# A hybrid encoder block on one core: which projection units are computed as seven half-size products, and what runs beside them

## The chip, the cores and the metric

The kernel runs on one core of a Trainium2 chip. The metric is the device time of one execution in microseconds (us), as the median of several runs. The engines are TensorE (PE, matmuls), VectorE (DVE), ScalarE (ACT), GpSimd (POOL) and SyncE (SP, here the queue that issues all DMAs). Each works through its own list of instructions in order and waits on semaphores for the others.

## The reference, cut to what matters

```python
h = rmsnorm(x, norm_w)                                   # 1024 tokens x 2048
q_a, k_a, v_a, g_a, q_r, k_r, v_r, g_r = split(h @ w_in) # 1024, 256, 256, 1024, 512, 512, 1024, 1024 columns
attn = windowed_attention(q_a, k_a, v_a, sink, rel_bias) # 16 heads of 64, window of 128
attn = rmsnorm(attn, attn_out_norm_w) * silu(g_a)
ret  = bidirectional_retention(rotary(q_r), rotary(k_r) / 8, v_r, decays)  # 8 heads, chunks of 128
ret  = head_groupnorm(ret, ret_gn_w) * silu(g_r)
x    = rmsnorm(x + concat(attn, ret) @ w_out, final_norm_w)
```

All is float32. The kernel splits each operand of the two large products into a high and a low part (float32r) and adds three matmuls, high x high, high x low and low x high.

## The kernel before, in words

The input projection is cut into units of 256 output columns for all 1024 tokens. There are 22: one of attention's keys (`ka`), one of its values (`va`), four of its queries (`qa`), four of retention's queries and keys (`qk`, 128 columns of each), four of retention's values (`vr`), four of attention's gates (`ga`) and four of retention's gates (`gr`).

The six units in `STD` (L26) are computed plainly (loop at L922): 16 steps over the inner dimension, at each four PSUM banks with three matmuls of 512 columns each (L973 to L975), 192 in all. The value unit has the tokens as the stationary operand and 256 columns as the moving one, so 384 matmuls (L966 to L968), and its result stands with tokens in the partitions. Units use the banks Ma and Mb, except the third and fifth, which use ST and O. `evac` (L852) takes a bank out of PSUM.

The 16 units in `FAST` (L27) are computed as seven half-size products in the manner of Strassen and Winograd: a half of the inner dimension is treated as a 2 x 2 block product, with combined tokens in `hT` and combined weights made on the fly. One pass over all 16 units takes the first half of the inner dimension, a second pass the second half (the loop at L1153, 32 half-units, each of seven slots p = 0 to 6 with 12 matmuls, L1035 to L1037, so 84). Slots of neighbouring units interleave: (q,0), (q-1,4), (q,1), (q-1,6), (q,2), (q-1,5), (q,3). For a slot `prep` splits weights (ACT the high part at L159, POOL the low part at L153), `prep_sums` combines them (on POOL in the first pass, on DVE in the second), and `collect` (L1050) takes the banks: bank a after products 0, 2, 4 and 5, b after 1, c after 4 and again after 6. In the first pass the first use of a bank is an ACT copy, in the second a DVE add to the partial sum, which the first pass stored to DRAM (`yd`) and which is loaded again. Between the passes `hT` is reloaded row by row (`c_load`, `c_split`).

A finished half-unit of the second pass goes through `deliver` (L1082). Gates get SiLU. Queries and keys are rotated (`rope`, L1105: a DVE shuffle, a POOL product, a DVE product, a DVE add), with two loads of cosine and sine. Values of retention are turned by four PE transposes into token order (`to_tokens`, L1123) and copied by ACT. Both are put off by a slot through the list `later`.

Everything else is done in pieces beside these matmuls. After every 3 matmuls of a product or bank (6 in a value unit), `point()` (L235) counts on; each `pace` points it runs one step of the queue `jobs` (attention's four groups, L494, then retention's four jobs, L648), each `apace` points one step of `aux` (bias copies, attn_sum, premix), and each point one step of `post`. Attention begins beside the last plain unit (L938) and goes on beside the first pass. Retention begins in the second pass, at slot 2 of its third unit (L1178). Its state chain is `kv` (L694, `scalar_tensor_tensor` at L156 into the tile ST). `premix` (L817) multiplies attention's gates with the norm's factors (POOL, L827) and its outputs (DVE, L830). The output projection follows in eight units (L1220), the first of them still beside retention's end.

A store is put off by seven points (`store`, L99) so that the SP queue does not wait for its data. Small tiles come from a ring of six (`t2`).

Of the kernel before, what the change touches and what calls it, by code (L numbers as in the profile page):

```python
# [21 lines left out]
NT2 = 6  # L22
# [14 lines left out]
def hybrid_block(ctx: ExitStack, tc: tile.TileContext, a: dict, out: bass.AP):  # L37
# [61 lines left out]
    def store(dst, src, t, then=None, delay=7):  # L99
# [5 lines left out]
        pend.append((pt[0] + delay, go, serial[t.name]))  # L105

    def held(t, bufs):
        tag, n = serial[t.name]

        return t  # L110

# [120 lines left out]

    pt, due, pace, adue, apace = [0], [0], [2.9], [0], [2.0]

# [242 lines left out]
    def q_post(i, tiles):  # L477
        for b, t in enumerate(tiles):
            et, hf = b // 2, b % 2
            for part in range(2):  # L480
                x = t2(F32R)
                if part == 0:
                    A.copy(x, t)
                    hi = x
                else:
                    tt(V, x, t, hi.bitcast(F32), ALU.subtract)
                last = (lambda: done.add(("qa", i))) if b == 3 and part else None
                store(qsd[2 * i + et, part, :, 512 * hf : 512 * hf + 512], x.bitcast(F32), x, last)
            yield

# [351 lines left out]
    def mixed_row():  # L842
# [6 lines left out]
        split(orow(row, 0), orow(row, 1), r)  # L849


    def evac(u, b, p, st):  # L852
        kind, i = STD[u]
        hf = b % 2
        d = t2()
        if kind == "va":
            for z in range(2):
# [4 lines left out]
                else:  # L862
                    A.activation(dz, pz, AF.Copy, scale=c)
            for z in range(2):
# [17 lines left out]
    def c_split(r):  # L882
        split(hT[:, r, 0:512], hT[:, r, 512:1024], held(staged.pop(r), NT2))

# [37 lines left out]
    for u, (kind, i) in enumerate(STD):  # L922
# [5 lines left out]
        for pos in range(NK):  # L928
# [29 lines left out]
            for b in range(4):  # L958
                p = banks[b]
                if kind == "va":  # L960
                    for z in range(2):
# [23 lines left out]
        elif kind == "qa":  # L985
            post.append((q_post(i, st), None))


# [50 lines left out]

    later = deque()  # L1040

    def partial(q, b):
# [36 lines left out]

    count = {}  # L1080

    def deliver(q, b):  # L1082
# [8 lines left out]
        def finished():  # L1091
            count[kind, i] = count.get((kind, i), 0) + 1
            if count[kind, i] == 4:
                done.add((kind, i))

        if kind in ("ga", "gr"):
            A.activation(t, t, AF.Silu)
            c = (0 if kind == "ga" else 8) + 2 * i + et
            store(gd[128 * c : 128 * c + 128, sl], t, t, finished)
        elif kind == "qk":  # L1100
            cs, sn = t2(), t2()
            SP.dma_start(cs, a["cos"][:, sl])
            SP.dma_start(sn, a["sin"][:, sl])

            def rope():  # L1105
                sh = t2()
                V.stream_shuffle(sh, t, [z ^ 1 for z in range(32)])
                tt(G, t, t, cs, ALU.mult)
                tt(V, sh, sh, sn, ALU.mult)

                def add():
                    tt(V, t, t, held(sh, NT2), ALU.add)
                    store(rqk[i, et, :, sl], t, t, finished)

                if q == NF:
                    add()
                else:
                    later.append(add)

            later.append(rope)  # L1120
        else:

            def to_tokens():  # L1123
                p = pT()
                for c in range(4):
                    T.transpose(p[:, 128 * c : 128 * c + 128], t[:, 128 * c : 128 * c + 128], ident)
                o = t2()
                A.copy(o, p)
                dst = vrd[i, :, 4 * hf : 4 * hf + 4, 128 * et : 128 * et + 128]
                store(dst, o.rearrange("p (c e) -> p c e", c=4), o, finished)  # L1130

            later.append(to_tokens)

# [19 lines left out]
    for n, (q, p) in enumerate(slots):  # L1153
# [8 lines left out]
        multiply(q, p)  # L1162
        now, ready_fns = later, list(later)
        later.clear()
        collect(q, p)
        for f in ready_fns:
            f()

# [7 lines left out]
        if q == NF - 1:  # L1176
            coming.extend(4 * p + j for j in range(4))
        if (q, p) == (NF + 2, 2):  # L1178
            drain(jobs, ("attn", 3))
# [5 lines left out]
            done.add("ret")  # L1185
            pace[0], apace[0] = 3.5, 3.0
            for g in range(4):
# [22 lines left out]
    assert mix_next[0] == 14, mix_next  # L1210
    while later:
        later.popleft()()
    while mixing:
# [235 lines left out]
```

## Time and profile before

| | |
|---|---|
| median of 3 runs | 1595.64 us (1592.18 to 1596.6) |
| profiled execution | 1595.88 us, its span 1594.1 us |
| mean granted clock of TensorE | 0.975 |
| DMA | 311.73 MB, mean 196 GB/s |

The span runs from the first to the last instruction; what lies around it is 1.8 us. A group's row gives line, engine, operation and tile, then busy time and the mean of one, then the idle time before it and what ended it. A row of the timeline begins with its start in us and its length; in brackets stands the idle time of the engine ahead of it and the releaser. PE's matmuls are pipelined: the length of one is longer than the distance of two starts.

### The profile page before, as it was taken

The page shows a single profiled execution, that of the slowest core. Times are in us where ns is not written, and L with a number is a line of the kernel's source. Part 1 is how long each engine was busy: PE and PEld are TensorE (multiplying, and loading weights), DVE is VectorE, ACT ScalarE, POOL GpSimd, SP SyncE. Part 2 cuts the span into 40 slices and gives each one's busy share as a digit, 9 for nine tenths or more (in the row PEclk, how much of TensorE's full clock was granted, in tenths as well). Part 3 has the DMA queues.
Part 4 walks back from the last instruction along what each step waited for, and adds up shares of the span by engine and source line. Part 5 has one row for each costly group of instructions (what it writes and reads, how often), then busy time and mean ns, then how long its engine had stood idle before and what let it go on. Part 6 is the DMA issues. An engine that isn't in the chain of part 4 may idle for free. (4 is left out here: it accounts for less than half of the span.)

```text
span 1594.1 us, 21805 instructions
## 1 busy us (share of the span) xinstructions
PE 1484.5 (93%) x7250; PEld 1237.2 (78%) x7250; DVE 923.5 (58%) x1880; ACT 668.1 (42%) x1417; POOL 591.0 (37%) x457
## 2 busy tenths in 40 slices
PE   8999998999999999998888698879998999999997
PEld 6998877887888888887777577657777787887886
DVE  6655446854564664577747856867667444364323
ACT  5311136764675675774332232222353343333210
POOL 3232221446556556445645545554442000113000
PEclk9999999999999999999999899989999999999999
DMA  8888668775455556357774675675464565566413
GB/s 302 300 268 296 243 187 276 244 235 161 139 160 154 159 162 189 115 160 247 242 232 142 201 242 175 219 252 163 155 230 150 173 224 185 159 206 199 135 35 106
DMA packets 195405, 311.73 MB, mean 196 GB/s; under 512 B 29355, under 2 KB 67243, under 8 KB 194652
## 3 DMA queue, kind: packets, MB, share of 16 engines
q1 hardware_dynamic: 195292, 310.33, 60.0%
q8 instruction: 57, 0.93, 0.3%
q14 instruction: 56, 0.46, 0.1%
HBM read 216.38 MB, written 93.88 MB: 195 GB/s over the span
## 5 line engine op out<-in xcount | busy, mean ns | idle before, releaser
L153 POOL TENSOR_TENSOR wl<-r,wh 128x512 fp32r<-128x512 f32 x224 | 298.7, 1337 | 318.9 <-ACT wh L159 308.3
L159 ACT CAST wh<-r 128x512 fp32r<-128x512 f32 x224 | 138.3, 619 | 194.4 <-PE psMa L1036 82.7
L1035 PE MATMUL psMa<-hT,wh 128*128 128x512 f32 x512 | 213.1, 416 | 5.8 <-DVE e L153 4.0
L1037 PE MATMUL psMa<-hT,wl 128*128 128x512 f32 x512 | 201.7, 394 | 2.3 <-POOL wl L153 2.3
L1035 PE MATMUL psMb<-hT,wh 128*128 128x512 f32 x384 | 166.0, 432 | 38.8 <-DVE e L153 38.7
L1036 PE MATMUL psMa<-hT,wh 128*128 128x512 f32 x512 | 201.0, 393 | 0.0
L159 ACT CAST wh<-e 128x512 fp32r<-128x512 f32 x160 | 97.9, 618 | 216.7 <-PE psMb L1254 78.7
L153 DVE TENSOR_TENSOR wl<-e,wh 128x512 fp32r<-128x512 f32 x112 | 84.6, 761 | 132.4 <-ACT wh L159 127.9
L1036 PE MATMUL psMb<-hT,wh 128*128 128x512 f32 x384 | 157.6, 410 | 0.0
L1037 PE MATMUL psMb<-hT,wl 128*128 128x512 f32 x384 | 157.2, 409 | 0.0
L153 POOL TENSOR_TENSOR wl<-e,wh 128x512 fp32r<-128x512 f32 x48 | 71.9, 1501 | 203.8 <-ACT wh L159 203.8
L1035 PEld LDWEIGHTS psMb<-hT,wh 128*128 128x128 f32 x384 | 77.4, 202 | 56.0 <-issue 32.2
L1035 PEld LDWEIGHTS psMa<-hT,wh 128*128 128x128 f32 x512 | 96.9, 189 | 24.6 <-issue 3.4
L1037 PEld LDWEIGHTS psMa<-hT,wl 128*128 128x128 f32 x512 | 96.7, 189 | 24.4 <-POOL wl L153 2.7
L560 DVE CUSTOM_DVE_ANT_0 P<-psST,bias,nsink 128x384 f32<-128x384 f32 (+1 forms) x128 | 74.1, 580 | 62.7 <-PE psST L552 62.4
L1036 PEld LDWEIGHTS psMa<-hT,wh 128*128 128x128 f32 x512 | 97.3, 190 | 16.0
L153 DVE TENSOR_TENSOR PTl<-psST,PTh 128x384 fp32r<-128x384 f32 (+1 forms) x128 | 66.7, 521 | 45.5 <-ACT PTh L604 42.4
L153 POOL TENSOR_TENSOR r<-r,r 128x512 f32<-128x512 f32 x64 | 85.0, 1329 | 20.8 <-DMA yd<-e 6.7
L159 ACT CAST hT<-t 128x512 fp32r<-128x512 f32 x100 | 60.6, 620 | 72.0 <-DMA t<-in_w_out 25.5
L1037 PEld LDWEIGHTS psMb<-hT,wl 128*128 128x128 f32 x384 | 76.8, 200 | 17.7
L564 ACT ACTIVATE P<-P,nmx 128x385 f32<-128x385 f32 (+1 forms) x128 | 76.1, 594 | 30.5 <-DVE nmx L560 28.9
L153 DVE TENSOR_TENSOR e<-psMb,e 128x512 f32<-128x512 f32 x96 | 65.6, 686 | 38.9 <-PE psMb L1037 32.4
(335 smaller groups left out, 3530.3 us busy)
## 6 DMA issues: line engine op xcount, KB each, us to landing
r<-in_w_fast SPq DMA_DIRECT2D x128, 256.0 KB, 2.8
e<-in_w_out SPq DMA_DIRECT2D x112, 256.0 KB, 2.9
yd<-e SPq DMA_DIRECT2D x64, 256.0 KB, 2.9
e<-yd SPq DMA_DIRECT2D x64, 256.0 KB, 3.5
t<-in_xT SPq DMA_DIRECT2D x31, 512.0 KB, 6.1
t<-cd SPq DMA_DIRECT2D x56, 256.0 KB, 4.3
e<-in_w_in SPq DMA_DIRECT2D x48, 256.0 KB, 4.7
md<-t SPq DMA_DIRECT2D x48, 256.0 KB, 2.8
```

What stands on the lines that cost most here:

```text
L153: eng.tensor_tensor(o, x, y, op)
L159: A.copy(o_hi, x)
L560: V.tensor_tensor_reduce(x[:, :W], p[:, :W], bias[2 * pr + c][:, k0 : k0 + W], -1.0, nsink[:, head : head + 1], ALU.add, ALU.min, nmx[:, c ...
L564: A.activation(x[:, : W + 1], x[:, : W + 1], AF.Exp, bias=nmx[:, c : c + 1], scale=-1.0, accum_out=sums[:, c : c + 1])
L1035: T.matmul(bank, wh[:, ws], hh, start=(j == 0 and p in (0, 1, 3)), stop=False, skip_group_check=True)
L1036: T.matmul(bank, wh[:, ws], hl, start=False, stop=False, skip_group_check=True)
L1037: T.matmul(bank, wl[:, ws], hh, start=False, stop=(j == 3), skip_group_check=True)
```

## The change

`qk` and `vr` move from `FAST` to `STD`. There are now 14 plain units and eight units of seven products, the gates alone, so 16 half-units instead of 32. The four `qk` units are plain with 192 matmuls, the four `vr` units like the value unit with 384 matmuls of 256 columns, in token order from the start, so that the transposes go. The rotation is a generator in the queue `post` (`rope_post`), with one load at a time through the single buffer e22; the store of retention's values stands in `evac`. Attention begins beside the same unit as before (`U_ATT`), now followed by eight more plain units, one step each 3.1 points instead of 2.9. Retention begins at slot 2 of the second half-unit of the first pass, one step each 3.3 points instead of 3.5, and premix takes a step each 2.0 points instead of 3.0. The parts of the diff:

```diff
 STD = [("ka", 0), ("va", 0), ("qa", 0), ("qa", 1), ("qa", 2), ("qa", 3)]
-FAST = []
 for _p in range(4):
-    FAST += [("qk", _p), ("vr", _p)]
-    FAST += [("ga", 2 * _p), ("ga", 2 * _p + 1)] if _p < 2 else []
-FAST += [("gr", _p) for _p in range(4)]
+    STD += [("qk", _p), ("vr", _p)]
+FAST = [("ga", _p) for _p in range(4)] + [("gr", _p) for _p in range(4)]
+U_ATT = 5
...
-    pt, due, pace, adue, apace = [0], [0], [2.9], [0], [2.0]
+    pt, due, pace, adue, apace = [0], [0], [3.1], [0], [2.0]
...
+    def rope_post(i, tiles):
+        for b, t in enumerate(tiles):
+            et, hf = b // 2, b % 2
+            sl = slice(512 * hf, 512 * hf + 512)
+            cs = et_("e22")
+            SP.dma_start(cs, a["cos"][:, sl])
+            for _ in range(4):
+                yield
+            sh = t2()
+            V.stream_shuffle(sh, t, [z ^ 1 for z in range(32)])
+            tt(G, t, t, cs, ALU.mult)
+            sn = et_("e22")
+            SP.dma_start(sn, a["sin"][:, sl])
+            for _ in range(5):
+                yield
+            tt(V, sh, sh, sn, ALU.mult)
+            tt(V, t, t, sh, ALU.add)
+            store(rqk[i, et, :, sl], t, t, lambda: one_more("qk", i))
+            yield
...
-        if kind == "va":
+        if kind in ("va", "vr"):
...
+            if kind == "vr":
+                dst = vrd[i, :, 2 * b : 2 * b + 2, :]
+                store(dst, d.rearrange("p (c e) -> p c e", c=2), d, lambda: one_more("vr", i))
...
-            if last_u and pos == 0:
+            if u == U_ATT and pos == 0:
...
-        if kind in ("ga", "gr"):
-            A.activation(t, t, AF.Silu)
-            c = (0 if kind == "ga" else 8) + 2 * i + et
-            store(gd[128 * c : 128 * c + 128, sl], t, t, finished)
-        elif kind == "qk":
...
-        else:
-
-            def to_tokens():
-                p = pT()
-                for c in range(4):
-                    T.transpose(p[:, 128 * c : 128 * c + 128], t[:, 128 * c : 128 * c + 128], ident)
...
+        A.activation(t, t, AF.Silu)
+        c = (0 if kind == "ga" else 8) + 2 * i + et
+        store(gd[128 * c : 128 * c + 128, sl], t, t, finished)
...
-        if (q, p) == (NF + 2, 2):
+        if (q, p) == (1, 2):
...
-            pace[0], apace[0] = 3.5, 3.0
+            pace[0], apace[0] = 3.3, 2.0
```

Two places in the order of the instructions. The first is PE beside attention. Before, in the first pass, attention's scores (L551, L552 into psST) and values (L582, L583 into psO) stand between two groups of three matmuls of a half-size product (L1035 to L1037):

```order
L1035 MATMUL psMb_2980<-hT,wh_2917 128x512
L1036 MATMUL psMb_2980<-hT,wh_2917 128x512
L1037 MATMUL psMb_2980<-hT,wl_2918 128x512
L551 MATMUL psST_2984<-k_314_2133,qj_2794 128x384
L552 MATMUL psST_2984<-k_315_2134,qj_2794 128x384
L582 MATMUL psO_2999<-PTh_2886,k_316_2135 128x256
L583 MATMUL psO_2999<-PTl_2887,k_316_2135 128x256
```

In the changed kernel the same (now L565, L566, and the transposes of the weights P, L611) stand between groups of a unit of retention's values (L991 to L993):

```order
L993 MATMUL psMb_3418<-wh_3879,hT 128x256
L565 MATMUL psST_4072<-k_619_3514,qj_3778 128x384
L566 MATMUL psST_4072<-k_620_3515,qj_3778 128x384
L611 MATMUL psST_4079<-ident,P_3900 128x128 x3
L991 MATMUL psMb_3419<-wh_3879,hT 128x256
L992 MATMUL psMb_3419<-wl_3880,hT 128x256
L993 MATMUL psMb_3419<-wh_3879,hT 128x256
```

Attention has moved from beside half-size products to beside plain units, whose matmuls here have 256 columns.

The second is DVE at retention's state chain (ST). Before, in the second pass, sums of weights (r) and adds of both banks (from psMa and psMb) stand among its steps:

```order
L156 SCALAR_TENSOR_TENSOR ST_8969<-ST_8969,cdec 64x128
L153 TENSOR_TENSOR e_1914_8937<-psMa_8680,e_1914_8937 128x512
L156 SCALAR_TENSOR_TENSOR ST_8969<-ST_8969,cdec 64x128
L153 TENSOR_TENSOR e_1914_8937<-psMb_8899,e_1914_8937 128x512
L156 SCALAR_TENSOR_TENSOR ST_8969<-ST_8969,cdec 64x128
L153 TENSOR_TENSOR r_8989<-r_8746,r_8989 128x512
L156 SCALAR_TENSOR_TENSOR ST_8969<-ST_8969,cdec 64x128
L153 TENSOR_TENSOR e_1905_8897<-psMb_9035,e_1905_8897 128x512
```

In the changed kernel the first chain stands in the first pass (L150 is the state step, L724 its copy, L147 the two-operand operations, sd retention's weighted scores):

```order
L150 SCALAR_TENSOR_TENSOR ST_8919<-ST_8919,cdec,psST_8914 64x128 x4
L147 TENSOR_TENSOR e_1604_8754<-psMb_8788,e_1604_8754 128x512
L147 TENSOR_TENSOR sd_8950<-psST_8945,dt_8798 128x512
L724 COPY ST_8919<-psST_8962 64x512
L150 SCALAR_TENSOR_TENSOR ST_8919<-ST_8919,cdec,psST_8962 64x128
L150 SCALAR_TENSOR_TENSOR ST_8919<-ST_8919,cdec 64x128
L150 SCALAR_TENSOR_TENSOR ST_8919<-ST_8919,cdec,psST_8962 64x128
L150 SCALAR_TENSOR_TENSOR ST_8919<-ST_8919,cdec 64x128
```

The adds from psMa and the sums of r are not on DVE there; the add from psMb is.

More of the change, by code (lines that the diff above doesn't have):

```diff
@@ L849, in mixed_row, with one_more @@
         split(orow(row, 0), orow(row, 1), r)
+    count = {}
+    def one_more(kind, i):
+        count[kind, i] = count.get((kind, i), 0) + 1
+        if count[kind, i] == 4:
+            done.add((kind, i))
     def evac(u, b, p, st):
@@ L863, in evac @@
                     A.activation(dz, pz, AF.Copy, scale=c)
-            for z in range(2):
+            for z in range(2) if kind == "va" else ():
                 store(
@@ L959, in hybrid_block @@
                 p = banks[b]
-                if kind == "va":
+                if kind in ("va", "vr"):
                     for z in range(2):
@@ L986, in hybrid_block @@
             post.append((q_post(i, st), None))
+        elif kind == "qk":
+            post.append((rope_post(i, st), None))
     raws, sums, ready_w, banks, outs = {}, {}, {}, {}, {}
```

38 lines of the change are left out of this document (2 added, 36 removed).

## The prediction

> **What bounds the kernel now.** I read the page's head first, then the table of stages, then the waits of the worst stage, then the timeline at its longest waits. The head gives span and busy time:
>
> ```profile
> span 1594.1 us, 21805 instructions
> PE 1484.5 (93%) x7250; PEld 1237.2 (78%) x7250; DVE 923.5 (58%) x1880; ACT 668.1 (42%) x1417; POOL 591.0 (37%) x457
> ```
>
> TensorE (PE) sets the time. Its busy time counts each matmul to its modelled end, so I take its pace from starts. The rows are the last matmul of the value unit and the first of the next plain unit, and that unit's last and its successor's first; then the first two of the value unit (256 columns each), and a run of four 128-column transposes with the matmul behind it:
>
> ```profile
> 101.82 0.28 PE L968 MATMUL psMb<-wh,r 128*128 128x256 f32 x1
> 101.94 0.40 PE L973 MATMUL psST<-hT,wh 128*128 128x512 f32 x1
> ...
> 145.26 0.39 PE L975 MATMUL psO<-r,wl 128*128 128x512 f32 x1
> 145.49 0.39 PE L973 MATMUL psMa<-hT,wh 128*128 128x512 f32 x1
> ...
> 52.56 0.28 PE L966 MATMUL psMa<-wh,hT 128*128 128x256 f32 x1
> 52.68 0.28 PE L967 MATMUL psMa<-wl,hT 128*128 128x256 f32 x1
> ...
> 1056.65 0.66 PE L1126 MATMUL psST<-ident,e 128*128 128x128 f32 x4 [1.22 <-DVE e L153]
> 1057.06 0.48 PE L1035 MATMUL psMa<-hT,wh 128*128 128x512 f32 x1
> ```
>
> A plain unit of 192 matmuls of 512 columns takes 145.49 - 101.94 = 43.55 us, 0.2268 us a matmul. A matmul of 256 columns takes 0.12 us, a transpose 0.41 / 4 = 0.10 us. Half a gate unit, one pass of seven products with 84 matmuls, needs 84 x 0.2268 = 19.05 us if nothing stands in the way.
>
> The table of stages has, in order: the value unit, a plain unit, the plain unit beside which attention begins, the first pass (16 half-units, beside attention), the first half-unit of the second pass, the whole second pass (beside retention), its last four half-units (gates only), the first output unit, and the rest. Columns are length, busy time of each engine, granted clock, DMA share and GB/s.
>
> ```profile
> 52.56:101.94 49.38, 49.25 (x403) 48.06 (x402) 33.07 (x44) 11.84 (x22) 18.32 (x10) 1.00 0.75 251
> 101.94:145.49 43.55, 43.55 (x194) 36.06 (x193) 17.92 (x25) 5.70 (x10) 10.75 (x8) 1.00 0.93 310
> 235.90:301.73 65.83, 60.96 (x313) 50.89 (x312) 45.16 (x116) 45.20 (x106) 11.72 (x9) 1.00 0.84 268
> 301.73:740.36 438.63, 423.50 (x2186) 360.08 (x2184) 252.73 (x655) 280.94 (x667) 244.42 (x187) 0.99 0.54 169
> 740.36:762.09 21.73, 19.37 (x84) 15.71 (x85) 19.29 (x24) 11.33 (x21) 13.66 (x10) 1.00 0.85 279
> 740.36:1213.60 473.24, 408.55 (x1961) 334.58 (x1962) 332.57 (x599) 155.90 (x296) 234.86 (x180) 0.94 0.63 206
> 1101.40:1213.60 112.20, 102.83 (x523) 85.28 (x522) 77.27 (x169) 48.59 (x93) 44.56 (x36) 0.97 0.55 183
> 1213.60:1274.10 60.50, 57.08 (x282) 46.80 (x281) 30.43 (x84) 21.82 (x43) 6.74 (x6) 0.97 0.50 158
> 1274.10:1594.10 320.00, 307.06 (x1345) 251.39 (x1343) 136.58 (x234) 96.61 (x194) 26.66 (x24) 0.99 0.48 156
> ```
>
> The second pass is the bad stage: PE stands idle for 473.24 - 408.55 = 64.7 us of it and is granted 0.94 of its clock, against 15.1 us and 0.99 in the first pass. DVE, not POOL, is the busiest helper there (70%). PE's waits in the second pass, by what it waited for (total, times, longest):
>
> ```profile
> PE psMb L1035 <- DVE e L153: 35.7, 9, 5.7
> PE psST L1126 <- DVE e L153: 22.5, 7, 7.7
> PE psMa L1035 <- DVE e L153: 4.0, 3, 2.8
> ```
>
> The first row is one place. Bank c is read by DVE after product 4 and written again by product 6, with only product 1 of the next half-unit between. When DVE has other work, PE stands. That work is retention's state chain, here ahead of a 5.70 us wait:
>
> ```profile
> 878.21 0.87 DVE L156 SCALAR_TENSOR_TENSOR ST<-ST,cdec 64x128 f32<-64x128 f32 x1
> 879.11 0.34 DVE L156 SCALAR_TENSOR_TENSOR ST<-ST,cdec,psST 64x128 f32<-64x128 f32 x1
> 879.48 0.35 DVE L156 SCALAR_TENSOR_TENSOR ST<-ST,cdec 64x128 f32<-64x128 f32 x1
> 879.87 0.69 DVE L153 TENSOR_TENSOR e<-psMa,e 128x512 f32<-128x512 f32 x1
> ...
> 880.97 0.69 DVE L153 TENSOR_TENSOR e<-psMb,e 128x512 f32<-128x512 f32 x1
> ...
> 881.81 0.77 PE L1035 MATMUL psMb<-hT,wh 128*128 128x512 f32 x1 [5.70 <-DVE e L153]
> ```
>
> **More matmuls.** Eight units become plain. Each saved 2 x 19.05 = 38.1 us as half-size products. Four query-key units now cost 43.55: 4 x 5.45 = 21.8 us more. Four value units cost 384 matmuls of 256 columns; 384 x 0.12 = 46.1 us by the starts, and the value unit's whole row, 49.38, is the upper end (19 other matmuls stand in it). I take 46.1: 4 x 8.0 = 32.0 us more. Their 64 transposes go: 64 x 0.10 = 6.6 us less. The sum is 47.2 us more work for PE, which nothing hides. The Trainium skill (TensorE: Matmul & The Clock Gate, Back-to-back issue gap) gives N / 2.4 ns plus about 2.5 ns from one warm matmul to the next: 215.8 ns for 512 columns, 109.2 for 256, so an estimate of 4 x 5.2 + 4 x 5.7 - 6.6 = 37 us. The rows' 226.8 and 120 ns are longer, and this chip's rows stand.
>
> **Attention beside plain units.** The stage ran from 235.90 to 740.36, 504.5 us: a plain unit, 16 x 19.05 = 304.8, and 156.1 left for attention's own matmuls with all delays. Attention's matmuls stay. What the half-size products added to the delays goes. Its prices are a bank wait, and the first matmul of each group of three, whose mean is 416 and 432 ns against 393 and 410 for the second:
>
> ```profile
> PE psMb L1035 <- DVE e L153: 6.2, 2, 3.2
> ...
> L1035 PE MATMUL psMa<-hT,wh 128*128 128x512 f32 x512 | 213.1, 416 | 5.8 <-DVE e L153 4.0 <-ACT e L1059 1.3 <-DVE bmv L748 0.5
> L1036 PE MATMUL psMa<-hT,wh 128*128 128x512 f32 x512 | 201.0, 393 | 0.0
> ```
>
> 448 groups in the first pass x 22 ns is 9.9, with 6.2 makes 16: 140 us stay. At best 25 go (131). At worst nothing goes and something comes: units follow one another on the same four banks, and the rotation (rope_post) puts 16 tiles of shuffle, product and add on DVE, with a POOL product and two loads through a single buffer between. A wait of that kind, in the second pass: a DVE operation 3.87 us late behind POOL, which was 5.50 us late behind a load:
>
> ```profile
> 961.17 1.29 POOL L153 TENSOR_TENSOR t<-t,t 128x512 f32<-128x512 f32 x1 [5.50 <-DMA t<-rbd]
> ...
> 962.49 1.77 DVE L156 SCALAR_TENSOR_TENSOR t<-t,ew,t 128x512 f32<-128x512 f32 x1 [3.87 <-POOL t L153]
> ```
>
> DVE is idle 42% of the first pass, so PE should see little of it; 1 us a tile as the upper end gives 156 + 16 = 172. As the order of PE in the section on the change shows, attention's pieces are the same; only what lies between them changes.
>
> Stage: 5 x 43.55 + 4 x 46.1 + 140 = 542.2 us, to 778.1.
>
> **Retention beside both passes.** Rotation, transposes and their stores leave these passes, and with them a wait on SP, whose queue holds the loads of weights and partial sums behind a store that waits for its data (SP's waits in the second pass); the rewritten store of retention's values now waits for its eviction beside attention, where weights are loaded 16 matmul groups ahead:
>
> ```profile
> SPq L101 <- ACT t L1128: 14.4, 7, 7.4
> ...
> r<-in_w_fast SPq DMA_DIRECT2D x128, 256.0 KB, 2.8
> ...
> yd<-e SPq DMA_DIRECT2D x64, 256.0 KB, 2.9
> e<-yd SPq DMA_DIRECT2D x64, 256.0 KB, 3.5
> ```
>
> Of the three kinds of transfers half go (64, 32 and 32 of 256 KB), and 64 loads of plain weights come, for a DMA share of 0.63: I cost that at nothing. The nearest row is the last four half-units before, gates with retention: 112.20 / 4 = 28.05 us each. About 13.5 half-units have retention beside them (four jobs of 29 steps, 3.3 points apart, 28 points to a half-unit). In the first pass DVE loses four sums and four adds a half-unit, as POOL makes the sums and ACT copies: in the order of DVE shown with the change, the adds from psMa and the sums of r are gone from between the state steps, the adds from psMb stay. Eight operations of 0.69 us are 5.5 us off DVE; I take 2 us of it for PE, 26.0 a half-unit, bounds 24.5 (midway between the 21.73 of the half-unit without retention and the first pass's mean, 438.63 / 16 = 27.4) and 29.6 (473.24 / 16). The pass: 6.7 x 26.0 + 6.8 x 28.05 + 2.5 without retention x 21.73 = 419.3. To this come 4 for reloading hT beside retention, 3 for the change from attention (the 2.8 us wait above), and 8 for premix, whose 16 pieces now stand two points a step instead of three, so that loads have less time (bounds 0 and 16). 434.3 us, to 1212. The bounds are 398 (24.5 and 26.0 a half-unit, and of the extras only the 3) and 481 (16 x 29.6, and 8). Retention then ends inside the pass, and the first output unit is plain: 43.55 + 1.5 = 45 instead of 60.50.
>
> **Sum.** 235.9 + 542.2 + 434.3 + 45 + 320.0 = 1577.4 us span. The profiled execution took 1595.88 us with a span of 1594.1, and the median of the runs is 1595.64, so the span lacks 1.8: 1579 us, 1.1% faster. A measurement of this kernel tells about 0.3% from nothing.
>
> **Rivals.** *Retention costs the same wherever it lies* (ends slower). The first pass gives POOL four sums more a half-unit. In the rows above a state step of 0.35 us took 0.87, and a three-operand product 1.77; undisturbed it takes 0.74:
>
> ```profile
> 861.73 0.74 DVE L156 SCALAR_TENSOR_TENSOR t<-t,ew,t 128x512 f32<-128x512 f32 x1
> L153 POOL TENSOR_TENSOR r<-r,r 128x512 f32<-128x512 f32 x64 | 85.0, 1329 | 20.8 <-DMA yd<-e 6.7 <-DMA r<-in_w_fast 6.4 <-issue 3.0
> ```
>
> If a POOL operation of 1.33 us holds DVE, the chain before bank c grows again by what the adds gave back: 16 x 29.6 + 8 = 481, 1626 us. It decides from about 28.3 us a half-unit with retention. The Trainium skill (SBUF — State Buffer, Who interferes with whom) says that a VectorE operation with two SBUF inputs and a GpSimd one that reads SBUF exclude each other for the whole instruction; the 0.74 and 1.77 us agree. 25%. *The plain units give it back*: attention keeps all its delays (156 us), 1595 us: 13%. For it speaks the rotation's single buffer, against it DVE's idle 42%. *Both stages run near their floor*: 131 and 398, 1534 us: 15%; for it speaks the 21.73 us of a half-unit without retention, against it the chain that stays. That the change does not do what it says is excluded by the order.
>
> **Numbers.** The forecast has 47%; of it 2 lie within 0.3%. Faster 0.45 + 0.15 = 0.60; within 0.3% 0.12 + 0.02 = 0.14; slower 0.25 + 0.01 = 0.26. The range, 1550 to 1618, leaves out the outer half of the floor rival and of the slower one.
>
> **What would show it.** Right: the stage from 235.9 ends near 778, half-units with retention last 26 to 28 us, the L1126 waits are gone, the psMb waits on DVE fall from 35.7 to some 20 us, the first output unit takes 45. Wrong: half-units over 28.3 in the first pass, or the attention stage past 795.

## The result and the profile after

The changed kernel takes 1647.4 us (median of 1642.42, 1647.4 and 1651.24; with one further, slow execution of 5238.3 us the median would be 1649.3), the kernel before 1593.9 us beside it. The ratio is 1.0334, with a 95% interval of 1.029 to 1.0379: slower by 53 us, where 1579 us was forecast, with a range of 1550 to 1618. The profiled execution took 1651.24 us, its span 1649.5.

```profile
span 1649.5 us, 23105 instructions
PE 1533.6 (93%) x8146; PEld 1310.8 (79%) x8146; DVE 840.6 (51%) x1800; ACT 625.6 (38%) x1337; POOL 480.7 (29%) x377
```

DVE lost 83 us of work (923.5 before), POOL 110, ACT 43. PE's 49 us more of busy time came through in full, and 6 more (by the spans). The table of stages of the changed kernel, with the columns of before: attention beside nine plain units, the last of these units, the first pass, in it half-units 2 to 7 (counted from 0; retention beside them), the second pass, in it half-units 8 to 14, and the first output unit.

```profile
237.40:807.60 570.20, 539.87 (x3474) 493.49 (x3472) 289.69 (x794) 269.95 (x660) 140.40 (x107) 0.97 0.50 154
736.80:807.60 70.80, 55.43 (x444) 54.52 (x442) 40.51 (x68) 30.62 (x61) 29.03 (x21) 0.90 0.76 242
807.60:1028.30 220.70, 199.36 (x989) 165.13 (x989) 102.90 (x237) 82.64 (x164) 133.86 (x107) 0.96 0.43 142
851.40:1028.30 176.90, 155.56 (x789) 128.87 (x787) 94.74 (x220) 66.01 (x132) 101.39 (x83) 0.96 0.42 138
1028.30:1277.70 249.40, 211.78 (x981) 169.43 (x982) 169.00 (x319) 96.23 (x185) 112.36 (x87) 0.92 0.67 222
1028.30:1249.60 221.30, 189.67 (x897) 151.91 (x897) 148.83 (x292) 81.88 (x161) 104.98 (x82) 0.93 0.64 211
1277.70:1327.50 49.80, 46.65 (x194) 37.82 (x193) 20.54 (x32) 16.65 (x30) 0.00 (x0) 0.93 0.60 192
```

| term | forecast | measured | surplus |
|---|---|---|---|
| to the start of attention | 235.9 | 237.4 | 1.5 |
| attention stage | 542.2 | 570.2 | 28.0 |
| both passes | 434.3 | 220.7 + 249.4 = 470.1 | 35.8 |
| first output unit | 45 | 49.8 | 4.8 |
| the rest | 320.0 | 322.0 | 2.0 |
| span | 1577.4 | 1649.5 | 72.1 |

Half-units 2 to 7 last 176.9 / 6 = 29.5 us (26.0 forecast), 8 to 14 last 221.3 / 7 = 31.6 (28.05, with 12 us of extras besides). All that is not plain, half-size or output matmuls at their own pace took, between the start of attention and the end of the first output unit, 504.5 + 533.74 - 696.7 = 341.5 us before, and takes 1090.1 - 750.5 = 339.6 now (the matmuls: 2 x 43.55 + 32 x 19.05 = 696.7, and 6 x 43.55 + 4 x 46.1 + 16 x 19.05 = 750.5). The forecast had it fall to 271. It did not fall: that is the whole error but 3.5 us. (6.6 us of the 341.5 were the transposes that went.)

What waited in both passes (engine, tile and line, what for; total, times, longest):

```profile
PE psMb L1062 <- DVE e L147: 27.9, 7, 7.4
DVE bnt L147 <- POOL bny L147: 24.5, 15, 6.5
DVE t L150 <- POOL t L147: 23.1, 8, 5.5
POOL t L147 <- DMA t<-rbd: 20.3, 7, 5.1
PE psMa L1062 <- ACT e L1084: 8.4, 2, 6.1
PE psMa L1062 <- DVE e L147: 8.2, 2, 6.4
```

The waits of L1126 are gone and psMb's fell from 35.7, both as forecast; others stand in their place. In the first pass, the timeline of POOL, DVE, ACT and PE about one of them:

```profile
915.53 1.29 POOL L147 TENSOR_TENSOR r<-r,r 128x512 f32<-128x512 f32 x1
916.89 2.39 POOL L147 TENSOR_TENSOR qs<-rq,qd 64x1024 f32<-64x1024 f32 x1
919.36 1.28 POOL L147 TENSOR_TENSOR r<-r,r 128x512 f32<-128x512 f32 x1
...
921.11 1.26 POOL L147 TENSOR_TENSOR wl<-r,wh 128x512 fp32r<-128x512 f32 x1
922.33 1.02 POOL L147 TENSOR_TENSOR bny<-bnv,mhalf 128x4 f32<-128x4 f32 x1
...
915.80 1.04 DVE L765 TENSOR_SCALAR bnv<-bmv 128x4 f32<-128x4 f32 x1
923.38 0.16 DVE L147 TENSOR_TENSOR bnt<-bnv,bny 128x4 f32<-128x4 f32 x1 [6.54 <-POOL bny L147]
...
924.43 0.88 ACT L777 ACTIVATE on<-on,bnt,bny 128x128 f32<-128x128 f32 x2 [8.38 <-DVE bnt L150]
...
926.46 0.57 ACT L1084 COPY e<-psMa 128x512 f32<-128x512 f32 x1
...
920.64 0.39 PE L1064 MATMUL psMb<-hT,wl 128*128 128x512 f32 x1
927.08 0.79 PE L1062 MATMUL psMa<-hT,wh 128*128 128x512 f32 x1 [6.05 <-ACT e L1084]
```

Four queues in a row: POOL's power for the group norm (bny, four columns) has its operand at 916.8 and stands behind a product (qs), a sum (r) and a split (wl) until 922.3; DVE waits for it 6.54 us with nothing else, ACT 8.38 us for DVE, ACT's copy of the bank stands behind, and PE waits 6.05 us for the bank. In the second pass premix does the like: POOL's product waits for a load, DVE for POOL, PE for the DVE add behind:

```profile
1146.44 1.26 POOL L147 TENSOR_TENSOR t<-t,t 128x512 f32<-128x512 f32 x1 [5.07 <-DMA t<-rbd]
...
1147.73 1.73 DVE L150 SCALAR_TENSOR_TENSOR t<-t,ew,t 128x512 f32<-128x512 f32 x1 [5.50 <-POOL t L147]
...
1150.21 0.77 PE L1062 MATMUL psMb<-hT,wh 128*128 128x512 f32 x1 [5.52 <-DVE e L147]
```

### The profile page after: what moved, and what is told of

Its sections match the earlier page's. It is cut to its first block, busy times and chain, and to the rows that moved or that the text cites. A ratio compares the mean times of both kernels' runs of the same rounds, so it can differ in the third digit from the quotient of the medians.

```text
span 1649.5 us, 23105 instructions
## 1 busy us (share of the span) xinstructions
PE 1533.6 (93%) x8146; PEld 1310.8 (79%) x8146; DVE 840.6 (51%) x1800; ACT 625.6 (38%) x1337; POOL 480.7 (29%) x377
## 4 chain that ended last, share of the span: by engine, by line
PE 52%; DMA 15%; DVE 12%; issue 10%; POOL 6%; ACT 3%; SPq 1%; POOLq 0%; ACTq 0%; DVEq 0%
DMA t<-gd 3%; POOL wl L147 2%; PE psMa L998 2%; PE psMa L999 2%; PE psMa L1000 2%; PE psMb L998 2%; PE psMb L999 2%; PE psMb L1000 2%; DMA e<-in_sin 2%; PE psMa L1062 2%; DVE ST L150 2%; DMA t<-cd 2%; PE psMa L1063 2%; PE psMa L1064 2%; PE psST L611 2%
## 5 line engine op out<-in xcount | busy, mean ns | idle before, releaser
L147 POOL TENSOR_TENSOR wl<-e,wh 128x512 fp32r<-128x512 f32 x112 | 155.7, 1392 | 519.5 <-ACT wh L153 509.6
L147 POOL TENSOR_TENSOR wl<-r,wh 128x512 fp32r<-128x512 f32 x112 | 149.8, 1341 | 171.2 <-ACT wh L153 164.3
L147 DVE TENSOR_TENSOR wl<-e,wh 128x512 fp32r<-128x512 f32 x112 | 84.2, 757 | 138.6 <-ACT wh L153 134.5
L1062 PE MATMUL psMa<-hT,wh 128*128 128x512 f32 x256 | 107.7, 421 | 22.6 <-ACT e L1084 8.4
L1062 PE MATMUL psMb<-hT,wh 128*128 128x512 f32 x192 | 83.7, 436 | 28.4 <-DVE e L147 27.9
L153 ACT CAST wh<-r 128x512 fp32r<-128x512 f32 x112 | 68.8, 618 | 104.6 <-PE psMa L1063 61.9
L1064 PE MATMUL psMa<-hT,wl 128*128 128x512 f32 x256 | 102.6, 401 | 0.0
L1063 PE MATMUL psMa<-hT,wh 128*128 128x512 f32 x256 | 102.6, 401 | 0.0
L147 DVE TENSOR_TENSOR PTl<-psST,PTh 128x384 fp32r<-128x384 f32 (+1 forms) x128 | 66.9, 523 | 51.5 <-ACT PTh L618 47.3
L147 DVE TENSOR_TENSOR hT<-t,hT 128x512 fp32r<-128x512 f32 x84 | 68.5, 832 | 40.7 <-ACT hT L153 39.0
L998 PE MATMUL psMa<-hT,wh 128*128 128x512 f32 x196 | 81.2, 414 | 6.2 <-DVE hT L287 6.2
L991 PE MATMUL psMa<-wh,hT 128*128 128x256 f32 x280 | 81.6, 291 | 0.0
L991 PE MATMUL psMb<-wh,hT 128*128 128x256 f32 x280 | 81.3, 290 | 0.0
L998 PE MATMUL psMb<-hT,wh 128*128 128x512 f32 x196 | 80.6, 411 | 0.0
L992 PE MATMUL psMb<-wl,hT 128*128 128x256 f32 x280 | 80.4, 287 | 0.0
L993 PE MATMUL psMb<-wh,hT 128*128 128x256 f32 x280 | 80.3, 287 | 0.0
L992 PE MATMUL psMa<-wl,hT 128*128 128x256 f32 x280 | 80.2, 287 | 0.0
```

The costliest lines, as they stand in the source:

```text
L147: eng.tensor_tensor(o, x, y, op)
L153: A.copy(o_hi, x)
L991: T.matmul(po, hh, wh[:, ws], start=first and z == 0, stop=False, skip_group_check=True)
L992: T.matmul(po, hh, wl[:, ws], start=False, stop=False, skip_group_check=True)
L993: T.matmul(po, hl, wh[:, ws], start=False, stop=last, skip_group_check=True)
L998: T.matmul(p, wh[:, ws], hh, start=first, stop=False)
```

## The experiments

Theory A: retention and premix cost PE time by what their own steps wait for, wherever they lie; what the change took off DVE was not what these waits ended on. Rivals: the change brought the waits (POOL's sums beside retention, steps of premix closer together); the attention stage's surplus is a matter of pace. Ratios are to the kernel before, timed beside it (its medians there 1596 to 1597 us), with 95% intervals. A number of us less or more is between medians, from 1649.3 for the changed kernel and from the median beside it for the kernel before. By the ratios some come out about 3 us smaller: 16 instead of 19 for the hold on group norm, 9 instead of 12 for premix's. An interval is 5 to 10 parts in 1000 wide, so a gain between two runs of the changed kernel is known to some 10 us only.

**Prices in both kernels: no retention.** ret_job only stores a constant tile; the rest stays.

```diff
-        for todo in (
...
-            for f, *args in todo:
-                f(*args)
-            yield
+        for n in range(26):
+            if n in (13, 17, 23, 25):
...
+                A.copy(so, gn)
...
+                store(md[e0 : e0 + 128, 512 * h : 512 * h + 512], so, so, last)
+            yield
```

In the kernel before:

> The kernel before without retention itself: each of its four jobs only writes a constant tile at the four places where it stored its output, so the outputs lack retention; rotation, transposes, premix and gates stay. Theory A (the delays belong to retention and premix and go with them wherever they are put): the second pass falls from 473 us to about 340 (304.8 for the products, 7 for transposes, some 28 for reloading hT, rotation and premix) and the first output unit to 46, so about 1446 us. Theory B (the forecast: a good part of the delays belongs to rotation, transposes and their stores): some 45 us of them stay without retention, about 1490 us.

In the changed kernel:

> The changed kernel without retention itself, in the same way. Theory A: the passes fall from 470 us to about 325, the whole to about 1500 us, so the changed kernel stays behind the one before by the 47 us of added matmuls and some 12 of attention's stage, 55 to 60 us, with retention or without. Theory B: without retention the kernel before keeps the delays of rotation and transposes, so the distance of the two shrinks to about 15 us.

Measured: 1479.8 us (0.9275, 0.9232 to 0.9319) and 1536.4 (0.9624, 0.959 to 0.9658). The distance, 57 us, is that with retention: retention costs 116 us before and 113 after. (The kernel before took 1596.2 us beside it.) Both levels lie 34 to 36 us above theory A's, since half-units without retention were not free of waits in the second pass; 1479.8 by itself is nearer to theory B's 1490. The distance decides: B had it shrink to 15 us. The table of stages of the changed kernel without retention, half-units 2 to 6, and 8 to 15:

```profile
853.10:948.30 95.20, 95.20 (x422) 78.87 (x421) 16.08 (x21) 35.32 (x62) 71.19 (x56) 1.00 0.37 118
969.20:1167.20 198.00, 167.56 (x673) 135.04 (x674) 109.80 (x130) 70.83 (x120) 92.27 (x71) 0.91 0.78 257
```

With POOL's sums but without retention a half-unit of the first pass takes 95.2 / 5 = 19.04 us, its bare matmuls. In the second, with reload, premix and the loads of mixed rows, it takes 198.0 / 8 = 24.75.

**No premix, in both.** The body of premix goes:

```diff
     def premix(kk):
-        for hf in range(2):
...
-            tt(G, g, g, n, ALU.mult)
...
+        yield
+        done.add(("pre", kk))
```

In the changed kernel:

> The changed kernel (1649 us) without premix: the 16 pieces with their three loads, POOL product, DVE product and store are left out, and the output projection takes attention's values without the norm's factors and gates. Theory A: premix and retention each cost PE time of their own. Without retention, half-units 8 to 15 still lost 45.7 us beyond their 19.05 us of matmuls, of it 9.0 in the last; so some 35 to 40 us go with premix, 1610 us, and half-units 9 to 14 last near 25 us. Rival R: retention alone fills these half-units, and premix lies beside it; they fall only to the 29.5 us of half-units 2 to 7, 15 us, 1634 us.

In the kernel before:

> The kernel before without premix, as was done to the changed one (which fell by 32 us, from 1649 to 1617). If premix costs the same in both, because in both its POOL product waits for a load and DVE for POOL: before falls by 28 to 36 us, to about 1563, and the distance to the changed kernel without premix stays near 54 us. Rival: before hid it, since its steps stood three points apart instead of two; then it falls by less than 12 us, to over 1584, and some 20 us of the 55 lost come from premix.

Measured: 1617.1 us (1.0129, 1.0099 to 1.0159), 32 us less, and 1555.6 (0.9763, 0.9724 to 0.9802), 41 less. Premix cost no less before. Half-units 8 to 14 of the changed kernel then take 189.3 / 7 = 27.0 us instead of 31.6:

```profile
1030.90:1220.20 189.30, 179.16 (x897) 147.69 (x897) 130.50 (x276) 83.75 (x164) 81.42 (x66) 0.97 0.50 165
```

**POOL's sums to DVE in the first pass** (changed kernel):

```diff
-        eng = V if q >= NF else G
+        eng = V
```

> The changed kernel with the sums of weights on DVE in both passes; only the engine of four additions a half-unit changes. Theory Q (in the first pass the group norm's power waits on POOL behind these sums, then DVE, then ACT's normalising, behind which ACT's copies of bank a stand): PE's waits for ACT's copy of bank a, 8.4 us, go, the half-units 2 to 7 fall from 29.5 us to about 27.5, and the whole by 8 to 14 us, to about 1637. Theory D (DVE's load before bank c is what costs): 32 more additions of 0.67 us on DVE make PE wait more for bank c, the same time or some 5 us more.

Measured: 1638.6 us (1.0266, 1.0227 to 1.0304), 11 us less, the waits bnt for bny 13.0 us with the longest 1.1. POOL's sums are part of the queue, but not all of it. (The intervals of this run and the changed kernel overlap.)

**Group norm's finish later in the source** (changed kernel): o_fin one step after its place in the list of steps.

```diff
-            ((o_fin, 0, 0), (o_mm, 0, 1, 0)),
-            ((o_mm, 0, 1, 1),),
+            ((o_mm, 0, 1, 0),),
+            ((o_fin, 0, 0), (o_mm, 0, 1, 1),),
```

> The changed kernel with o_fin one step later behind its o_mm (twice one step, the last one step later too), so that POOL's power for the group norm has 3.3 points more before DVE stands waiting for it. Theory Q (PE waits on ACT, ACT on DVE's group norm, DVE on POOL's small power queued behind sums of weights): the DVE waits bnt <- POOL bny of 24.5 us nearly go, half-units 2 to 7 fall from 29.5 to about 28, and the time by 12 to 20 us, to some 1633. Rival: the steps only stand elsewhere in the same full queues; within 5 us of 1649.

Measured: 1647.1 us (1.0328, 1.0298 to 1.0357), the bnt waits 26.5 us. This was no test. In DVE's order the step (bnt from bnv and bny, L147) stands where it stood, first as the 1034th of DVE's 1800 instructions in either trace, directly behind the operation that makes bnv for POOL (L765). The scheduler that makes the queues from the source put it back. So the next run holds it by an edge, behind the last add and copy issued so far.

**Group norm's finish held in the order, in both** (on top of the later place of the run before, which alone changed nothing):

```diff
+            with tc.issue_after(last_on["V"]), tc.issue_after(last_on["A"]):
                 newton(t, v, y)
```

In the changed kernel:

> The changed kernel with o_fin one step later, and this time held in the order of DVE and ACT behind the last collecting add and copy (the same shift in the source alone had left DVE's wait at its row). Theory Q (PE waits on ACT's copies, ACT on DVE's group norm, DVE on POOL's small power behind sums): the waits bnt <- POOL bny of 24.5 us fall below 8, PE's wait at psMa for ACT in the first pass (8.4 us) goes, 12 to 18 us less, 1631 to 1637. Rival: these waits stand beside others of the same length; within 5 us of 1649.

In the kernel before:

> The kernel before with the hold on group norm's finish alone. In before, retention lies only beside the second pass, where DVE makes the sums of weights and POOL is less loaded, so POOL's power should come in time: within 6 us of 1594, and nearly all of the 26 us that before won with both holds is premix's. If instead the group norm's wait stood there as in the changed kernel: 10 to 19 us less, about 1580.

Measured: 1630.1 us (1.0235, 1.019 to 1.0279), 19 us less; and 1576.9 (0.9883, 0.9847 to 0.9919), 20 less. The wait fell as expected. The changed kernel with the hold, in both passes:

```profile
DVE bnt L149 <- POOL bny L149: 7.1, 8, 1.6
PE psMb L1065 <- DVE e L149: 15.4, 6, 5.3
```

The kernel before as it was, in the second pass:

```profile
DVE bnt L153 <- POOL bny L153: 17.5, 13, 3.5
```

The kernel before with the hold, there:

```profile
PE psMb L1038 <- DVE e L155: 12.4, 7, 5.1
DVE bnt L155 <- POOL bny L155: 5.8, 5, 2.1
```

That the queue behind this step costs time is shown by removal. But the second expectation failed: the kernel before gains as much. The group norm's queue did not come with the change, and of the 35.7 us of psMb's waits that the prediction put to the state chain, 23 went with it.

**Premix held in the order** (changed kernel; 5 and 4 points from the loads to POOL's product and on to DVE's, instead of 4 and 4), and both holds in both kernels:

```diff
+            with tc.issue_after(last_on["G"]):
                 tt(G, g, g, n, ALU.mult)
...
+            with tc.issue_after(last_on["V"]):
                 stt(V, r, r, ew[:, kk : kk + 1], g, ALU.mult, ALU.mult)
```

> The changed kernel with premix's POOL product held behind the last POOL operation issued 5 points after the loads, and its DVE product behind the last DVE operation 4 points later; the same 10 points a piece as before. If the 32 us that went without premix are waits for its loads (POOL t <- DMA 26 us, DVE t <- POOL t 23 us): they fall to a third, and the time by some 15 to 20 us, to about 1632. Rival: they are the work itself (a POOL product of 1.3 us that stops splits, a DVE product of 0.75 to 1.77 us, and 48 loads and 16 stores): within 6 us of 1649.

The kernel before with both holds:

> The kernel before with the same two holds on the order (group norm's finish, premix). If these waits stand in before as well, and were not brought by the change: 20 to 30 us less, about 1568, and the distance to the changed kernel with the same cures stays 40 us or more, about the added matmuls. Rival: they are the changed kernel's own (POOL's sums beside retention, premix at two points a step): within 5 us of 1594, and the cured changed kernel comes near it.

The changed kernel with both:

> The changed kernel with the two holds on the order (group norm's finish, premix) and nothing else. The run with three cures came to 1636, because the late sums shortened the last plain unit by 10 us and then kept retention's start waiting, 17 us in the gates' first two half-units. If the two holds add (19 and 12 us alone): 1615 to 1621. If they share what they free: 1626 to 1632. Beside before with the same holds (1570) the distance should then be 45 to 60 us, the added 47 us of matmuls and more.

Measured: premix alone 1637.0 us (1.0276, 1.0227 to 1.0324), 12 less, though the interval overlaps with the changed kernel's; the waits fell to

```profile
DVE t L152 <- POOL t L149: 11.4, 3, 8.5
POOL t L149 <- DMA t<-rbd: 1.4, 1, 1.4
```

The kernel before with both: 1570.3 (0.9841, 0.98 to 0.9882), the fastest of all here. The changed kernel with both: 1636.5 (1.0248, 1.0211 to 1.0284), no better than either alone. Its trace shows other waits in the place of those that went. PE's waits for DVE at psMb fell from 27.9 to 8.9 us, but retention's transposes, which need the output of the held step, now wait 19.2 us for ACT (4.0 in the changed kernel, 12.3 with the first hold alone), and the last half-unit 9.5 us for a row of hT:

```profile
PE psST L787 <- ACT on L780: 19.2, 9, 7.7
```

No run took these out.

**Stores of gates later** (changed kernel), so that SP's queue waits less for ACT:

```diff
-        store(gd[128 * c : 128 * c + 128, sl], t, t, finished)
+        store(gd[128 * c : 128 * c + 128, sl], t, t, finished, 14)
```

> The changed kernel with the store of a finished gate bank put off by 14 points instead of 7. In the second pass the SP queue waits 53.5 us (25 times) at stores for ACT's SiLU, and the loads of premix, partial sums and weights stand behind. If SP's waiting makes the loads late on which POOL and then DVE wait (POOL t <- DMA t<-rbd 20.3 us, DVE t <- POOL t 23.1 us): the SP wait falls below 15 us, those two waits to half, and the time by 10 to 15 us, to about 1637. Rival: the loads have slack or wait for tiles; within 4 us of 1649.

Measured: 1646.6 us (1.0322, 1.028 to 1.0364). SP's wait there only fell to 46.4 us, so the run tells little.

**Attention's pace 2.9 again** (changed kernel):

```diff
-    pt, due, pace, adue, apace = [0], [0], [3.1], [0], [2.0]
+    pt, due, pace, adue, apace = [0], [0], [2.9], [0], [2.0]
```

> The changed kernel with attention at one step each 2.9 points, as in the kernel before, instead of 3.1, so attention ends 36 points earlier. Theory S (attention's norm stands too close behind its last sums, so PE waits 12.2 us for POOL's sum of squares at the end of the last plain unit): that wait goes, about 12 us less, 1637. Theory D (attention beside plain units loses by its density): denser steps cost as much as the wait gives, the same time within 4 us.

Measured: 1655.5 us (1.0373, 1.0337 to 1.0408). The wait for POOL fell only from 12.2 to 8.1 us, and 9.5 us for ACT's emptying of a bank came beside it. A denser pace does not free the end of the stage.

**The end of the attention stage.** There PE waited 12.2 us for POOL's sum of squares (attn_norm). Two runs put that step off, first by 8 steps in the source:

```diff
     def attn_norm():
+        for _ in range(8):
+            yield
```

> The changed kernel with attn_norm put off by 8 steps of the queue (about 25 points, 17 us), so that its matmuls stand behind the last sum of squares of POOL and the wait PE psST <- POOL acc (12.2 us, twice, in the last plain unit) has nothing to wait for. If that wait holds the stage: 1637 to 1641 us, and the last plain unit falls from 70.8 us to about 60. Rival: another wait ends as late at that place (the pace experiment only moved the time to evictions), and the time stays within 4 us of 1649.

then by an edge behind the gates' third slot:

```diff
+        with tc.issue_after(mark["f0"]):
             for t in range(8):
                 T.matmul(
```

> The changed kernel with the matmuls of attn_norm held in PE's order behind the third slot of the gates' first half-unit (putting the step 8 steps later in the source had left them at the same place of PE's order, at the end of the last plain unit). If the wait for POOL's acc is PE's alone: the 12.6 us there go, and the time falls to 1637 to 1641. Rival: the gates' first slots wait as long for the rows of hT whose loads go out on the same queue until 802 us; within 4 us of 1649.

Measured: 1648.6 us (1.0329, 1.0304 to 1.0354) and 1647.6 (1.034, 1.0296 to 1.0384). The first left the matmuls where they were in PE's order, between the last plain matmul and the first half-size one; no test again. The second moved it, and PE's wait turned into another of the same length:

```profile
PE psMa L1065 <- ACT t L886: 14.7, 1, 14.7
```

L886 empties the last value unit's bank. In ACT's order the squares of attention's last sums stood ahead of it. Their loads (t from mpd) stand on SP among 28 loads of hT's new rows (t from cd), all into the same ring of six tiles. SP's queue in the changed kernel:

```profile
791.58 0.87 SPq L629 DMA_DIRECT2D t<-mpd  x2
792.73 1.96 SPq L905 DMA_DIRECT2D t<-cd  x4
...
798.69 0.87 SPq L629 DMA_DIRECT2D t<-mpd  x2
```

A round of one sum's two loads and four rows takes 7.1 us. So the next run takes the last sums out of that unit:

```diff
-                    aux.append((after(attn_sum(g), ("attn", g)), None))
+                    aux.append((after(attn_sum(g), ("attn", g), *(("f0",) if g == 3 else ())), None))
```

> The changed kernel with the last group's sums of attn_sum begun only after the gates' first slot, so that the 28 loads of hT's new rows (c_load) and their splits have the ring of six tiles, SP, ACT and DVE to themselves in the last plain unit. When the matmuls of attn_norm were put off alone, PE waited 14.7 us for ACT's evacuation of that unit's bank, which stood behind squares of attn_sum that waited for their loads. If the ring is what holds the stage's end: the last plain unit falls from 70.8 us to 56 to 60, the time to 1634 to 1638. Rival: the reload alone (28 loads, splits on ACT and DVE) holds it as long; within 5 us of 1649.

Measured: 1655.1 us (1.0364, 1.0322 to 1.0405). The last plain unit, and then half-units 0 and 1, in this kernel:

```profile
736.30:796.70 60.40, 51.87 (x428) 51.04 (x427) 36.14 (x65) 28.15 (x58) 20.70 (x15) 1.00 0.73 227
796.70:857.60 60.90, 50.99 (x217) 41.30 (x218) 13.92 (x20) 19.10 (x38) 37.73 (x30) 0.89 0.51 169
```

The unit fell from 70.8 to 60.4 us. Moving attn_norm alone had left it at 69.5 (733.3 to 802.8 in that run), so the last sums did hold it; whether by the ring of tiles or by their own work on ACT and DVE is not told apart. The gates' first two half-units rose from 43.8 (851.4 - 807.6) to 60.9: by the source, sums, attn_norm and retention's opening follow each other, so they only ended later. The 10 us were there, and were given back with 6 more.

**All cures at once** (changed kernel): late sums and both holds; and POOL's sums on DVE besides.

> The changed kernel with three cures at once: sums of attention's last group late, group norm's finish held in the order (19 us alone), premix held in the order (12 us alone). If they are separate queues of waits: 19 + 12 + 12 = 43 less, 1606, still above the 1594 of before, since 47 us of matmuls were added. Rival: they share what they free; 1615 to 1625.

> The changed kernel with the three cures and the sums of weights on DVE in the first pass too (11 us alone). If the sums cost by holding POOL's power of the group norm, their 11 us are in the cure already: within 4 us of the kernel with three cures. If they cost by holding POOL's splits or DVE besides: 5 to 10 us less than it.

Measured: 1635.8 us (1.0241, 1.0194 to 1.0288) and 1634.6 (1.0242, 1.0201 to 1.0283). The cures do not add up: three together (1635.8) are no faster than the first hold alone (1630.1). That the sums' 11 us are missing there too does not show that they are the same as the hold's 19, since premix's 12 add nothing either.

The distances together, medians in us:

| | before | changed | distance |
|---|---|---|---|
| as they are | 1593.9 | 1647.4 | 53 |
| no retention | 1479.8 | 1536.4 | 57 |
| no premix | 1555.6 | 1617.1 | 62 |
| group norm held | 1576.9 | 1630.1 | 53 |
| group norm and premix held | 1570.3 | 1636.5 | 66 |

Whatever is taken out of both, the changed kernel stays 53 to 66 us behind: the 47 us of added matmuls and some more.

## Why the prediction was wrong, point by point

- **More matmuls, 47.2 us**: right. The matmuls of the new plain units kept the forecast pace (120 ns from start to start at 256 columns, 228 to 236 at 512, medians of the attention stage), and nothing hid them. By the Trainium skill's formula (TensorE: Matmul & The Clock Gate, Back-to-back issue gap) it would have been an estimate of 37 us. These starts speak for the rows; the distances of 53 to 66 us hold other terms too.
- **"What the half-size products added to the delays goes"** (attention stage, 140 us): the step that failed first. Of the 16 us, 9.9 were read from the length of a group's first matmul, 416 ns against 393. That time is real, but it belongs to attention and not to the half-size products. It is paid behind attention's transposes of 128 columns, where the next matmul of 512 columns is 0.48 us long and its successor starts 0.32 us later instead of 0.23. In the kernel before 113 groups of the first pass stood right behind such transposes. In the changed kernel 128 groups of the plain units do. At 0.08 to 0.09 us each that is some 10 us in both. In a plain unit without attention all three matmuls of a group last 389 ns. A place in a plain unit beside attention, in the changed kernel:

```profile
301.83 0.38 PE L611 MATMUL psST<-ident,P 128*128 128x128 f32 x2
301.96 0.48 PE L998 MATMUL psMb<-hT,wh 128*128 128x512 f32 x1
302.28 0.39 PE L999 MATMUL psMb<-hT,wh 128*128 128x512 f32 x1
302.51 0.40 PE L1000 MATMUL psMb<-hT,wl 128*128 128x512 f32 x1
```

The other 6.2 us went, and more came: 12.2 at the end of the stage and 12.7 at the beginnings of attention's groups, where before had 1.3 and 2.0 (L551 and L597). So 168.0 us stayed (570.2 - 5 x 43.55 - 4 x 46.1), 28 more than forecast and 12 more than before. No run here won the first of these back: moved, it gave way to others as long. The second was not tried. PE's waits in the stage:

```profile
PE psST L646 <- POOL acc L147: 12.2, 2, 7.0
PE psST L565 <- DVE nmx L574: 7.7, 4, 2.3
PE psST L611 <- DVE nmx L574: 5.0, 3, 2.5
```

- **"I take 2 us of it for PE, 26.0 a half-unit"**: 29.5. The four sums and four adds did leave DVE, but DVE was busy for only 94.74 of the 176.9 us of half-units 2 to 7, and stood waiting for POOL. With that one step held in the order these half-units take 27.9 us (167.5 / 6).
- **"8 for premix (bounds 0 and 16)"**: 32. The row of 28.05 us came from half-units that premix had already left (the last four of before), and premix's 41 us in the half-units ahead of them were not looked for. So 28.05 became 31.6. A bound of 16 had no row behind it.
- **The rivals.** "Retention costs the same wherever it lies" holds in its name: 116 and 113 us. Its mechanism, a POOL operation that lengthens the chain before bank c, is in the trace, but small. In half-units 2 to 7 the state steps with both inputs in SBUF last 352 ns in the median and up to 1341, the long ones beside a POOL operation; that is 7.4 us more for all 24 (15.8 - 24 x 0.352). The steps that read PSUM besides keep their 339:

```profile
L150 DVE SCALAR_TENSOR_TENSOR ST<-ST,cdec 64x128 f32<-64x128 f32 x24 | 15.8, 659 | 0.8
```

PE waited only 5.8 us at psMb for DVE in that whole pass, and the hold cut these waits in both passes from 27.9 to 15.4 us with the sums still on POOL. So POOL mattered more through the order of its queue, before the change too. Moving the sums to DVE takes away part of both, and its 11 us do not tell them apart. "The plain units give it back" came true as well, and 12 us beyond. The two were priced one at a time, 1626 and 1595; together they make 1577.4 + 16 + 46.7 = 1640 us of span, near the 1649.5, but in part by luck, since the 46.7 were worked out from the smaller of the two mechanisms.

What stays open: how the changed kernel could keep what both holds free, and what brought the longer waits at the beginnings of attention's groups.

## What to carry to other kernels

Work taken off a helper engine buys time only where a wait of the bound engine ends on that work; price a stage by leaving it out of the kernel before, in which it can be done as well, and not by the load of an engine. Take a duration from a stretch that has the same company: a row without premix says nothing of a half-unit with it, a mean over matmuls hides what stood ahead of the long ones, and two rivals that do not exclude each other are added. Where a scheduler makes the queues, read the order of the instructions after each edit of the source: two edits here left the instruction where it was, and only an edge moved it.

## What the runs showed of the hardware

A wait can cost more than its length. After the 6.05 us wait at 927 the matmuls start 0.43 us apart instead of 0.2268, at a granted clock of 0.51, for some 3 us. The timeline of PE, and the table of stages for that stretch (granted clock third from the end):

```profile
927.67 0.63 PE L1063 MATMUL psMa<-hT,wh 128*128 128x512 f32 x1
928.10 0.63 PE L1064 MATMUL psMa<-hT,wl 128*128 128x512 f32 x1
...
930.49 0.48 PE L1062 MATMUL psMa<-hT,wh 128*128 128x512 f32 x1
930.80 0.39 PE L1063 MATMUL psMa<-hT,wh 128*128 128x512 f32 x1
931.03 0.39 PE L1064 MATMUL psMa<-hT,wl 128*128 128x512 f32 x1
```

```profile
927.00:930.50 3.50, 3.42 (x11) 2.74 (x11) 0.00 (x0) 1.07 (x3) 2.80 (x3) 0.51 0.29 109
```

Six of these matmuls at 0.2 us more, and four transposes behind them, make about 1.6 us on top of the wait (930.49 - 927.08 = 3.41, where six times 0.2268 and 0.41 are 1.77), which no row of waits shows. The Trainium skill (TensorE: Matmul & The Clock Gate, HAM oscillation — how this bites in real kernels) says that an idle gap of more than about 3.4 us throttles the clock to half. The trace agrees for this wait. It does not show where the limit lies: a wait of 3.15 us at 1286.61 in the changed kernel was followed by starts 0.43 us apart too, and one of 2.82 us at 780.52 in the kernel before by starts 0.23 us apart.
